# Two-stream feed forward: every low part of the weights on the vector engine, and gate times up written to PSUM

## Chip, cores and metric

One Trainium2 chip, one of its NeuronCores. The metric is the device time of one execution, in microseconds (us), as the median of some runs. The engines are called as the profile calls them: PE (TensorE, matmuls; PEld its weight loads), DVE (VectorE), ACT (ScalarE), POOL (GpSimd) and SP (SyncE, whose queue issues the DMAs).

## The reference, cut to what matters

Two small networks run one after the other on a latent sequence and a context sequence ("streams") of 256 tokens and 1024 features each. Between norms, a convolution module, three attentions and a state space mixer, each has four feed forward layers. In float32:

```
def _swiglu(h, wg, wu, wd):
    return (jax.nn.silu(h @ wg) * (h @ wu)) @ wd          # 1024 -> 2816 -> 1024

def _ffn_half(s, mod, g, wg, wu, wd):
    shift, scale, gate = mod
    h = _modulate(_rmsnorm(s, g), shift, scale)
    return s + 0.5 * gate * _swiglu(h, wg, wu, wd)
...
    ml = (jax.nn.silu(c) @ mod_w[i] + mod_b[i]).reshape(B, 1, N_MOD, D)   # the modulation vectors
```

The state space mixer of the second network needs input, output and transition matrices that depend on weights alone.

## The kernel before

**Split numbers.** A float32 product is made of three matmul passes over rounded operands. Every operand is split into a high part (a rounded copy, made by ACT) and a low part (the number minus its high part, a subtraction). So each weight tile `raw` that arrives by DMA becomes `wh` (ACT, L180) and `wl` (L185), and each activation tile has two parts too: `hh`/`hl` for the input of a layer, `Hh`/`Hl` for the product of gate and up.

**Weight stream.** `pump` runs ahead of PE: it issues the DMA of a chunk of two pieces (L161, on SP's queue), the conversion `wh`, and, when the next piece is converted or the piece is needed, `wl` of the piece before. Five pieces have room. A piece is converted as soon as PE is done with the one five before it. Which engine makes `wl` is decided by the piece's number: every second one by POOL, the others by DVE:

```
            eng = nc.gpsimd if self.n_cv % self.cvm == 1 or self.cv_behind else nc.vector
            self.low()
            self.low_p = lambda eng=eng, l2=l2, r=r, h2=h2: eng.tensor_sub(l2, r, h2.bitcast(F32))
```

**Feed forward** (`ffn`). The 22 tiles of 128 hidden features stand in three groups (6, 8 and 8). In each group PE first makes the gate and up tiles (`gu`, two PSUM tiles for each hidden tile: 48 matmuls over 512 columns, both streams at once), then eight `pd` tiles of the down projection, which read all `Hh` and `Hl` of the group. Between them stands `glu`:

```
                    nc.scalar.activation(out=sg[:, :n], in_=pg[:, :n], func=AF.Silu)
                    pr = sg
                    nc.vector.tensor_mul(pr[:, :n], sg[:, :n], pu[:, :n])
                    hi = Hh[f0 + i][:, c0:c0 + n]
                    nc.scalar.activation(out=hi, in_=pr[:, :n], func=AF.Copy)
                    nc.vector.tensor_sub(Hl[f0 + i][:, c0:c0 + n], pr[:, :n], hi.bitcast(F32))
```

The lines are L774 (`Silu`, ACT), L776 (product, DVE), L778 (`Hh`, ACT) and L779 (`Hl`, DVE). Five PSUM tiles `m` are shared by `gu` and `pd`.

**The eight feed forwards** are called f100, f102, f110 and f112 (first network) and f200, f202, f210 and f212 (second). f112 and f212 have one stream and 256 columns; the other six have two streams.

**Work beside it.** While PE runs a feed forward, DVE makes the modulation vectors of later layers: `jk` (L535), a custom product with a sum over a piece `mw` of the modulation weights. In f100, f102 and f110 the first steps of the state space mixer (`s5_pre`, "the side work") run as well: POOL multiplies small matrices `w` (L2014 to L2024, L2040 to L2050), PE transposes or multiplies them (`pvt`, `kp`), ACT copies them, SP writes them to memory (`dV`), and a later step reuses the buffer. The steps of both are handed out by the matmul time that the program counts, not by what an engine has done. Each engine works through its queue in order. Tile, the framework, orders the instructions of each engine by a simulated run of its own and puts in the waits.

Of the kernel before, what the change touches and what calls it, by code (L numbers as in the profile page):

```python
# [13 lines left out]
D = 1024  # L14
# [13 lines left out]
def pipe(n, stages, lag=1):  # L28
    """stage i of item k goes out lag * i items later, so that no engine stands behind the one before it"""
    for t in range(n + lag * (len(stages) - 1)):  # L30
        for i, f in enumerate(stages):
            if 0 <= t - lag * i < n:
                f(t - lag * i)
# [28 lines left out]
class Task:  # L62
    """background work, one step of a generator every `period` ns of PE time; a step yields the least wait after it"""
# [11 lines left out]
class Core:  # L75
# [39 lines left out]
    def behind(self, ins, prev):  # L115
        """ins is not to be issued before prev"""
        self.tc.add_manual_dep(ins.ins, prev.ins.name, mybir.DependencyInfo(
            mybir.DependencyClass.NoSync, mybir.DependencyReason.DATA), reason="order")

    def behind_pe(self, ins):  # L120
        """ins is not to be issued before the tensor engine has come to where the program is now"""
        self.tc.add_manual_dep(ins.ins, self.last_mm.ins.name, mybir.DependencyInfo(
            mybir.DependencyClass.NoSync, mybir.DependencyReason.DATA), reason="pace")
# [43 lines left out]
    def pump(self):  # L167
        while self.n_cv < min(len(self.pieces), self.n_rel + NBUF):
# [14 lines left out]
            eng = nc.gpsimd if self.n_cv % self.cvm == 1 or self.cv_behind else nc.vector  # L183
# [28 lines left out]
    def gemm(self, out, w, rhs, ks, start=True, stop=True):  # L212
        """w=(hi,lo) pieces [128,nk,128]; rhs(k)->(hi,lo) APs; ks: list of (piece index, rhs key)"""
# [26 lines left out]
    def rstd(self, ch, acc, ncol, eps, cb, d1=900, d2=1500, inv=None, parts=False, pin=0):  # L240
        """acc [128, 128*ncol]: sums over feature tiles, or, parts, the means over each of them in PSUM; cb(bc) with bc [128, 128*ncol] in PSUM."""
# [57 lines left out]
def cols(v):  # L299
    """[n*128] -> [128, n]"""  # L300
# [3 lines left out]
def tiles(w):  # L304
    """[K, M] -> [MT, 128(k), KT, 128(m)]"""
# [53 lines left out]
def na_bias(rpb):  # L359
    """[16, 15, 31] -> [16, 128, 2, 256]: the bias of query (qt, p) and key, -1e30 outside the column window"""  # L360
# [10 lines left out]
def pairs(w):  # L371
    """[K, M] -> [MT/2, 128, 2*KT*128]"""
# [4 lines left out]
def halves(w):  # L377
    """[K, 2M]: tile m of the first half beside tile m of the second -> [MT, 128, 2*KT*128]"""
# [8 lines left out]
def layout(a):  # L387
# [64 lines left out]
    # state space: partition (group parity, state), columns (direction, group pair)  # L452
# [10 lines left out]
    # rows (half, group mod 4, tile in half, group half, h)  # L463
# [5 lines left out]
class Net(Core):  # L469
# [39 lines left out]
    def mods(self, specs):  # L509
        """specs: (b, l, columns, streams_of, then); the sums of every column, then() after the last; a step per sum"""  # L510
# [36 lines left out]
    def begin(self, room):  # L547
        """the first norm, as a generator: feature tile k of both streams goes into hh / hl at step k, as soon as its
        modulation is there; the scale by the vector engine, the shift by the tensor engine"""
# [106 lines left out]
    def prep_norm(self, b, l, n, s):  # L656
        """G = g * (1 + scale)"""
# [43 lines left out]
    def plan_ffn(self, b, l, i, head=0, tail=0):  # L701
        """head, tail: gate/up tiles at the start and down chunks at the end that pass by once for each stream"""
# [12 lines left out]
    def ffn(self, b, streams, ready, gate, after, nsplit=4, first=1, work=None, side=None, head=0, tail=0, begin=None):  # L715
        """ready[s]: chain that fills hh/hl; gate[s]: [128,8] factors; after(s): called once x[s] is done
        (block 1) or y[s] with its sums of squares is done (block 2)."""
        nc, tc = self.nc, self.tc
        two = len(streams) == 2
        N = 512 if two else T  # L720
        with ExitStack() as es:
# [29 lines left out]
            def products(ws, c0, n, last=True, outer=None, step=None):  # L751
                """the gate and up tiles f0, f0 + 1, ... of columns c0:c0 + n; k goes through all of them in turn"""
# [18 lines left out]
            def glu(ps, f0, c0, n):  # L771
                for i, (pg, pu) in enumerate(ps):
                    sg = fp.tile([128, 512], F32, tag="sg", name="sg", bufs=2)
                    nc.scalar.activation(out=sg[:, :n], in_=pg[:, :n], func=AF.Silu)  # L774
                    pr = sg
# [26 lines left out]
            for g, (f0, nf) in enumerate(FGROUPS):  # L802
# [40 lines left out]
                if lastg:  # L843
                    if task is not None:
                        self.drain(task)
                    if side is not None:
                        self.stop(side)
                        self.cvm = 2
# [18 lines left out]
    def proj(self, streams, rhs, epi, ready, after, nk=KT, tiles=1, n=KT, first=1, last=4, again=0):  # L867
        """n outputs of `tiles` weight pieces each; epi(i, s, [psum...]); the first `first` and last `last`
        outputs run one stream after the other, the others for both at once."""
# [49 lines left out]
    def first_tiles(self, ready, streams, n=5):  # L919
        """the first n output tiles, for one stream after the other; gives (j, PSUM tile) as each is done"""  # L920
# [25 lines left out]
    def conv(self, ready, gate, after, NPE=5, NPOOL=8, L=1, n1_=12, n2_=7):  # L946
# [3 lines left out]
        with self.pool("conv") as cp:  # L950
# [23 lines left out]
            def taps(m, ss, n_pe=NPE, n_pool=NPOOL):  # L974
                """v[m]: the taps spread over the tensor engine, the vector engine, and scalar with GpSimd"""
# [171 lines left out]
    def weave(self, a, ta, b, tb, lead=0.0):  # L1147
        """run two generators in turn, in proportion to their PE times ta and tb, b behind a by the part lead"""
# [20 lines left out]
    def na(self, ready, gate, after, NR=1.1, NL=0.2):  # L1169
        nc, tc = self.nc, self.tc  # L1170
        with self.pool("na") as np_, self.pool("na2", 2) as n2:
# [51 lines left out]
            def produce():  # L1223
                """q and k of two heads and, every other time, v of four; at the end the output projection"""
# [32 lines left out]
                # what needs the lat rows only, then the rest of k and v  # L1257
# [34 lines left out]
                # the first output tiles over the heads that are done  # L1292
# [37 lines left out]
            def scores(h, qt, pt, bt):  # L1330
                """softmax of one head and query tile, in pt[:, qt] (SBUF, [128 q, 512 keys])"""
# [26 lines left out]
            def turn(pt, c):  # L1358
                """transpose keys c, c + 1 (of 128) of pt [128 q, 2, keys] into hi and lo [128 keys, q]"""
# [63 lines left out]
    def sums_on_pe(self, n=T):  # L1423
        """a function that takes the squares of feature tile k, and the PSUM tile of its means for rstd"""
# [7 lines left out]
    def post_norm(self, s, acc, gp, sums="vector"):  # L1432
        """x += gp * y * rstd(y); returns the chain and the sums of squares of the new x"""
# [43 lines left out]
    def attn2(self, ready, finish):  # L1477
        """finish(s, acc): y[s] and its sums of squares are done"""
        nc, tc = self.nc, self.tc
        S2 = (LAT, CTX)  # L1480
        with ExitStack() as es:
# [42 lines left out]
            def pe_rope(ps):  # L1524
                """rope of rows 64:96 of ps, with the swapped halves in 96:128, in place"""
# [10 lines left out]
            def rope64(ps):  # L1536
                """rope of both heads' lat columns, in place; rows (half, head)"""
# [8 lines left out]
            # latent projections, then the window attention's q, k, v  # L1546
# [64 lines left out]
            def unit(H, u, ps, p, w, msk):  # L1611
                """exponentials of scores ps [128, w, keys] into p (SBUF), each of the w rows by itself, and their sums"""
# [38 lines left out]
            def score(H, u):  # L1651
                """u = 0, 1: the lat queries of a tile against every key; 2: the ctx queries against the ctx keys"""
# [29 lines left out]
            def pv(H, c):  # L1682
                """the products with the high parts of chunk c, then those with the low parts of the one before"""
# [789 lines left out]
```

## Time and profile before

| | before |
|---|---|
| median of 3 runs (lowest to highest) | 3812.37 us (3811.04 to 3816.39) |
| span of the profiled execution | 3809.8 us |
| mean granted clock of PE | 0.959 |
| PE busy | 3512.7 us (92%) |
| DVE busy | 2733.4 us (72%) |
| ACT busy | 1428.2 us (37%) |
| POOL busy | 1742.2 us (46%) |
| `wl` on POOL | 340 pieces, 2604 ns each |
| `wl` on DVE | 339 pieces, 1422 ns each |
| `Hl` on DVE | 196 tiles, 1482 ns each |
| gate times up on DVE | 196 tiles, 570 ns each |

Busy time is the union of an engine's instructions, and a share is of the span. PE has the largest share, so its idle time, and the stretches in which it runs at a lower granted clock, are what can still be taken out. The profiled execution has no time of its own beside its span; the span lies 2.6 us below the median of the runs.

### The profile page before, as it was taken

To read this page: it belongs to the slowest core of one execution; us is meant where nothing else is said; L and a number is where in the kernel's file an instruction comes from. 1 tells how busy PE (TensorE), PEld (TensorE's weight loads), DVE (VectorE), ACT (ScalarE), POOL (GpSimd) and SP (SyncE) were. 2 spreads that over 40 slices of the span, in tenths; PEclk is the share of its full clock that TensorE was granted. 3 is DMA by queue.
4 is the path that set the end of the run, shared out by engine and by line. 5 is a ranking of instruction groups with operands and counts; after the bars stand their busy time and mean duration, and the time that the engine had idled before them with its cause. 6 is when DMAs were issued, how large, how long until landed. Compare 5 with 4: busy or idle time off the path is not lost. (4 is left out here: it accounts for less than half of the span.)

```text
span 3809.8 us, 55159 instructions
## 1 busy us (share of the span) xinstructions
PE 3512.7 (92%) x21110; PEld 3061.6 (80%) x21110; DVE 2733.4 (72%) x4128; ACT 1428.2 (37%) x2500; POOL 1742.2 (46%) x1255
## 2 busy tenths in 40 slices
PE   8889977899998988998999999888999999998798
PEld 7667755888887776898898888778888888886798
DVE  8889699676659786777998676696666633367665
ACT  4222354533233222455444223465322432233443
POOL 6777556367656676412443223334222422234343
PEclk9999988899999999999999999999999999998899
DMA  6555410255445854423665553102455332238353
GB/s 231 175 193 189 147 55 34 95 170 167 159 142 186 290 198 162 145 95 118 237 238 189 187 177 123 62 28 91 170 183 193 144 111 89 99 122 276 108 183 131
DMA packets 158127, 580.42 MB, mean 152 GB/s; under 512 B 25252, under 2 KB 56740, under 8 KB 118184
## 3 DMA queue, kind: packets, MB, share of 16 engines
q1 hardware_dynamic: 157864, 576.91, 43.6%
q8 instruction: 166, 2.72, 0.3%
q14 instruction: 97, 0.79, 0.1%
HBM read 547.55 MB, written 29.29 MB: 151 GB/s over the span
## 5 line engine op out<-in xcount | busy, mean ns | idle before, releaser
L185 POOL TENSOR_TENSOR wl<-raw,wh 128x1024 fp32r<-128x1024 f32 (+1 forms) x340 | 884.7, 2604 | 1443.7 <-ACT wh L180 1360.9
L180 ACT ACTIVATE wh<-raw 128x1024 fp32r<-128x1024 f32 (+1 forms) x679 | 700.4, 1037 | 1222.5 <-PE gu L106 531.3
L106 PE MATMUL gu<-hl,wh 128*128 128x512 f32 (+1 forms) x3136 | 1085.5, 347 | 9.3 <-DVE hl L693 7.5
L106 PE MATMUL gu<-hh,wl 128*128 128x512 f32 (+1 forms) x3136 | 1084.6, 347 | 8.6 <-DVE wl L185 5.2
L106 PE MATMUL gu<-hh,wh 128*128 128x512 f32 (+1 forms) x3136 | 1080.5, 348 | 7.1 <-ACT hh L690 6.8
L535 DVE CUSTOM_DVE_ANT_0 jk<-mw,cb,vec 128x1024 bf16<-128x1024 f32 x480 | 760.4, 1584 | 38.7 <-DMA mw<-in_mw_dram 24.8
L106 PEld LDWEIGHTS gu<-hl,wh 128*128 128x128 f32 x3136 | 600.7, 192 | 83.9 <-DVE hl L693 9.9
L106 PEld LDWEIGHTS gu<-hh,wl 128*128 128x128 f32 x3136 | 600.4, 192 | 81.8 <-DVE wl L185 6.0
L185 DVE TENSOR_TENSOR wl<-raw,wh 128x1024 fp32r<-128x1024 f32 (+1 forms) x339 | 482.1, 1422 | 252.3 <-ACT wh L180 235.9
L106 PEld LDWEIGHTS gu<-hh,wh 128*128 128x128 f32 x3136 | 598.2, 193 | 80.3 <-ACT hh L690 8.4
L106 PE MATMUL pd<-Hh,wh 128*128 128x256 f32 (+1 forms) x1696 | 567.6, 337 | 24.9 <-ACT Hh L778 23.1
L106 PE MATMUL pd<-Hl,wh 128*128 128x256 f32 (+1 forms) x1696 | 569.3, 336 | 8.4 <-DVE Hl L779 8.4
L106 PE MATMUL pd<-Hh,wl 128*128 128x256 f32 (+1 forms) x1696 | 568.6, 336 | 2.3 <-POOL wl L185 1.9
L106 PEld LDWEIGHTS pd<-Hh,wh 128*128 128x128 f32 x1696 | 326.4, 193 | 59.7 <-ACT Hh L778 26.7
L106 PEld LDWEIGHTS pd<-Hl,wh 128*128 128x128 f32 x1696 | 327.1, 193 | 42.9 <-DVE Hl L779 11.5
L106 PEld LDWEIGHTS pd<-Hh,wl 128*128 128x128 f32 x1696 | 327.6, 193 | 33.7 <-POOL wl L185 2.3
L779 DVE TENSOR_TENSOR Hl<-sg,Hh 128x512 fp32r<-128x512 f32 (+1 forms) x196 | 290.4, 1482 | 45.2 <-ACT Hh L778 45.2
L776 DVE TENSOR_TENSOR sg<-sg,gu 128x512 f32<-128x512 f32 (+1 forms) x196 | 111.6, 570 | 281.2 <-PE gu L106 264.1
L106 PE MATMUL pj<-hh,wh 128*128 128x256 f32 (+1 forms) x736 | 229.6, 328 | 22.1 <-ACT t L967 10.7
L778 ACT ACTIVATE Hh<-sg 128x512 fp32r<-128x512 f32 (+1 forms) x196 | 105.3, 537 | 343.7 <-DVE sg L776 343.3
L106 PE MATMUL pj<-hh,wl 128*128 128x256 f32 (+1 forms) x736 | 230.2, 317 | 0.8 <-DVE wl L185 0.8
L106 PE MATMUL pj<-hl,wh 128*128 128x256 f32 (+1 forms) x736 | 230.0, 317 | 0.6 <-DVE hl L693 0.6
(407 smaller groups left out, 4738.7 us busy)
## 6 DMA issues: line engine op xcount, KB each, us to landing
raw<-in_gu_dram SPq DMA_DIRECT2D x186, 1024.0 KB, 4.8
mw<-in_mw_dram SPq DMA_DIRECT2D x280, 512.0 KB, 4.1
raw<-in_dn2b_dram SPq DMA_DIRECT2D x38, 1024.0 KB, 4.8
raw<-in_dn1b_dram SPq DMA_DIRECT2D x32, 1024.0 KB, 5.5
raw<-in_dn1a_dram SPq DMA_DIRECT2D x16, 768.0 KB, 4.9
raw<-in_pw_dram SPq DMA_DIRECT2D x12, 1024.0 KB, 4.7
raw<-in_dn2a_dram SPq DMA_DIRECT2D x16, 768.0 KB, 4.2
dV<-w SPq DMA_DIRECT2D x32, 256.0 KB, 4.3
```

The costliest lines, as they stand in the source:

```text
L106: ins = self.last_mm = self.nc.tensor.matmul(out=out, lhsT=lhsT, rhs=rhs, start=start, stop=stop, **kw)
L180: ins = nc.scalar.activation(out=h2, in_=r, func=AF.Copy)
L185: self.low_p = lambda eng=eng, l2=l2, r=r, h2=h2: eng.tensor_sub(l2, r, h2.bitcast(F32))
L535: self.behind_pe(nc.vector.tensor_tensor_reduce(out=jk, in0=tl[i], in1=self.cb[s], scale=1.0, scalar=self.V(f"mod_b{b}{l}")[:, j:j + 1], o ...
L776: nc.vector.tensor_mul(pr[:, :n], sg[:, :n], pu[:, :n])
L778: nc.scalar.activation(out=hi, in_=pr[:, :n], func=AF.Copy)
L779: nc.vector.tensor_sub(Hl[f0 + i][:, c0:c0 + n], pr[:, :n], hi.bitcast(F32))
```

## The change

Two edits. In a feed forward of two streams `cvm` is 0, so that every `wl` made while it runs is DVE's; at the end of the last group, ahead of its last pieces, `cvm` is 2 again, and pieces alternate as before. And the product of gate and up is written over `pu`, in PSUM, from where `Hh` and `Hl` are made; this holds for one stream too. Comments and docstrings went as well, which moves some lines by one (L776 is L777 in the changed kernel, L779 is L780).

```diff
-            eng = nc.gpsimd if self.n_cv % self.cvm == 1 or self.cv_behind else nc.vector
+            eng = nc.gpsimd if (self.cvm and self.n_cv % self.cvm == 1) or self.cv_behind else nc.vector
...
     def ffn(self, b, streams, ready, gate, after, nsplit=4, first=1, work=None, side=None, head=0, tail=0, begin=None):
         nc, tc = self.nc, self.tc
         two = len(streams) == 2
         N = 512 if two else T
+        self.cvm = 0 if two else 2
...
-                    pr = sg
+                    pr = pu
                     nc.vector.tensor_mul(pr[:, :n], sg[:, :n], pu[:, :n])
...
                     if side is not None:
                         self.stop(side)
-                        self.cvm = 2
+                    self.cvm = 2
```

The first place is POOL's queue in f110, where the side work makes the matrices `w_11007` and `w_11008` for the products `kp`. Before:

```order
L2024 TENSOR_TENSOR w_10818<-w_10818,w_10819 128x512
L185 TENSOR_TENSOR wl<-raw,wh 128x1024 x2
L2042 TENSOR_TENSOR w_11009<-pw_10677,bc 128x576
L2046 TENSOR_TENSOR w_11008<-pw_10677,bc 128x576
L185 TENSOR_TENSOR wl<-raw,wh 128x1024
L2040 TENSOR_TENSOR w_11007<-pw_10676,bc 128x576
L2044 TENSOR_TENSOR w_11007<-w_11007,w_11009 128x576
```

And in the changed kernel:

```order
L2025 TENSOR_TENSOR w_10818<-w_10818,w_10819 128x512
L2043 TENSOR_TENSOR w_11009<-pw_10677,bc 128x576
L2047 TENSOR_TENSOR w_11008<-pw_10677,bc 128x576
L2041 TENSOR_TENSOR w_11007<-pw_10676,bc 128x576
L2045 TENSOR_TENSOR w_11007<-w_11007,w_11009 128x576
```

The three low parts that stood between the steps are gone; the steps themselves stand in the same order.

The second place is DVE's queue in the second group of f100, from one product of gate and up to the low part of its tile and on to the next product. Before:

```order
L776 TENSOR_TENSOR sg<-sg,gu 128x512
L185 TENSOR_TENSOR wl<-raw,wh 128x1024
L535 ISA jk,mod_211<-mw,cb_245,vec 128x1024
L535 ISA mod_211 128x1
L779 TENSOR_TENSOR Hl_703<-sg,Hh_695 128x512
L535 ISA jk,mod_212<-mw,cb_275,vec 128x1024
L535 ISA mod_212 128x1
L535 ISA jk,mod_211<-mw,cb_245,vec 128x1024
```

In the changed kernel:

```order
L777 TENSOR_TENSOR gu<-sg,gu 128x512
L535 ISA jk,mod_212<-mw,cb_275,vec 128x1024
L535 ISA mod_212 128x1
L185 TENSOR_TENSOR wl<-raw,wh 128x1024
L780 TENSOR_TENSOR Hl_703<-gu,Hh_695 128x512
L535 ISA jk,mod_211<-mw,cb_245,vec 128x1024
L535 ISA mod_211 128x1
...
L185 TENSOR_TENSOR wl<-raw,wh 128x1024
L535 ISA jk,mod_212<-mw,cb_275,vec 128x1024
L535 ISA mod_212 128x1
```

Each hidden tile now has two low parts of weights in DVE's queue in place of one; one `jk` and one `wl` stand between the product and `Hl`, as before.

The third place is DVE's queue near the end of the first group of f100, around `cx`, which overwrites a tile that POOL's powers (`cth`, L1879) read. Before:

```order
L776 TENSOR_TENSOR sg<-sg,gu 128x512
L185 TENSOR_TENSOR wl<-raw,wh 128x768
L535 ISA jk,mod_212<-mw,cb_275,vec 128x1024
L535 ISA mod_212 128x1
L779 TENSOR_TENSOR Hl_707<-sg,Hh_699 128x512
L1925 TENSOR_TENSOR cx<-cli 128x64
```

In the changed kernel:

```order
L780 TENSOR_TENSOR Hl_706<-gu,Hh_698 128x512
L535 ISA jk,mod_211<-mw,cb_245,vec 128x1024
L535 ISA mod_211 128x1
L185 TENSOR_TENSOR wl<-raw,wh 128x768
L535 ISA jk,mod_212<-mw,cb_275,vec 128x1024
L535 ISA mod_212 128x1
L1926 TENSOR_TENSOR cx<-cli 128x64
```

`cx` stands one hidden tile earlier: behind the low part of the group's fourth tile, where it stood behind that of its fifth.

## Rows read from the trace of the kernel before

**Rows 1.** Windows: stretches of f100, f102 (twice), f110, f112, f212.

```profile
core 0: us, PE busy (x) PEld busy (x) DVE busy (x) ACT busy (x) POOL busy (x), PEclk, DMA share, GB/s
110.00:474.70 364.70, 322.42 (x1507) 262.59 (x1505) 297.93 (x450) 92.92 (x138) 251.50 (x199) 0.94 0.52 175
743.20:1126.20 383.00, 377.78 (x2028) 322.12 (x2027) 249.99 (x374) 124.60 (x189) 246.28 (x230) 1.00 0.49 161
819.40:1126.20 306.80, 303.81 (x1499) 253.61 (x1498) 188.42 (x286) 89.50 (x127) 193.80 (x179) 1.00 0.49 161
1126.20:1561.80 435.60, 391.35 (x2034) 328.49 (x2033) 347.14 (x474) 124.26 (x190) 295.47 (x257) 0.95 0.57 199
1779.90:1995.00 215.10, 201.84 (x1592) 198.94 (x1592) 195.24 (x244) 94.12 (x144) 91.92 (x35) 0.95 0.61 220
3605.60:3797.30 191.70, 191.69 (x1584) 191.48 (x1584) 114.70 (x111) 86.64 (x130) 73.44 (x31) 0.99 0.44 154
```

**Rows 2.** PE's waits in f100 from 110 us: us in total, times, longest.

```profile
PE pd L106 <- ACT Hh L778: 14.2, 3, 7.6
PE kp L106 <- POOL w L2044: 8.2, 3, 4.6
PE kp L106 <- POOL w L2050: 5.6, 2, 4.0
PE pd L106 <- DVE Hl L779: 5.0, 3, 2.6
PE pvt L106 <- POOL w L2024: 4.0, 2, 2.3
```

**Rows 3.** PE's waits in f110.

```profile
PE kp L106 <- POOL w L2050: 12.6, 3, 6.7
PE kp L106 <- POOL w L2044: 10.1, 2, 7.7
PE pvt L106 <- POOL w L2018: 9.4, 2, 7.4
```

**Rows 4.** DVE by line in f110: count, busy us, mean ns, idle before.

```profile
L535 DVE CUSTOM_DVE_ANT_0 jk<-mw,cb,vec 128x1024 bf16<-128x1024 f32 x112 | 180.2, 1609 | 32.0 <-DMA mw<-in_mw_dram 22.2 <-ACT cb L506 7.8 <-DVE mod L535 0.5
L185 DVE TENSOR_TENSOR wl<-raw,wh 128x1024 fp32r<-128x1024 f32 x32 | 50.1, 1566 | 0.6 <-ACT wh L180 0.5
L779 DVE TENSOR_TENSOR Hl<-sg,Hh 128x512 fp32r<-128x512 f32 x18 | 28.5, 1582 | 4.5 <-ACT Hh L778 4.5
L776 DVE TENSOR_TENSOR sg<-sg,gu 128x512 f32<-128x512 f32 x18 | 12.3, 681 | 14.6 <-PE gu L106 14.6
```

**Rows 5.** The same view of f200.

```profile
L535 DVE CUSTOM_DVE_ANT_0 jk<-mw,cb,vec 128x1024 bf16<-128x1024 f32 x96 | 140.6, 1465 | 1.4
```

**Rows 6.** POOL by line in f110.

```profile
L185 POOL TENSOR_TENSOR wl<-raw,wh 128x1024 fp32r<-128x1024 f32 (+1 forms) x37 | 104.4, 2825 | 59.1 <-ACT wh L180 58.9
```

**Rows 7.** POOL by line in f200, whose three small groups are left out.

```profile
L185 POOL TENSOR_TENSOR wl<-raw,wh 128x1024 fp32r<-128x1024 f32 (+1 forms) x39 | 104.4, 2679 | 247.8 <-ACT wh L180 239.3 <-DVE Hl L779 3.3 <-DVE wl L185 3.0
```

**Rows 8.** All instructions on tile `jk`: ns min/median/max, first and last start.

```profile
L535 DVE CUSTOM_DVE_ANT_0 jk<-mw,cb,vec x480: 1267/1283/3495, 66.6 to 2949.3; 128x1024 bf16<-128x1024 f32 x160
```

**Rows 9.** Timeline of DVE in f110, while POOL is idle: start, us.

```profile
1324.76 1.22 DVE L185 TENSOR_TENSOR wl<-raw,wh 128x1024 fp32r<-128x1024 f32 x1
```

**Rows 10.** Timeline of POOL in f110; idle time before and its releaser in brackets.

```profile
1331.65 1.17 POOL L2042 TENSOR_TENSOR w<-pw,bc 128x576 f32<-128x576 f32 x1 [12.88 <-DMA dV<-w]
...
1333.89 3.32 POOL L185 TENSOR_TENSOR wl<-raw,wh 128x1024 fp32r<-128x1024 f32 x1
1337.18 2.14 POOL L2040 TENSOR_TENSOR w<-pw,bc 128x576 f32<-128x576 f32 x1
```

**Rows 11.** Timeline of DVE in f100.

```profile
113.92 0.25 DVE L1925 TENSOR_TENSOR cx<-cli 128x64 f32<-128x64 f32 x1 [10.53 <-POOL cth L1879]
```

**Rows 12.** Timeline of POOL in f100.

```profile
90.20 6.17 POOL L185 TENSOR_TENSOR wl<-raw,wh 128x1024 fp32r<-128x1024 f32 x2
...
99.05 14.85 POOL L1879 TENSOR_TENSOR cth<-cx,cr 128x8 f32<-128x8 f32 x8
```

**Rows 13.** DVE by line in f112.

```profile
L779 DVE TENSOR_TENSOR Hl<-sg,Hh 128x256 fp32r<-128x256 f32 x22 | 29.0, 1318 | 0.0
```

## The prediction, made before the result was known

> **What bounds the kernel now.** I first took the busy shares: PE leads with 92%, so the time is PE's work, its waits and its clock. Then I looked at each feed forward by itself, since the edits act there alone. Stretches of PE time are read in the windows view [rows 1]. f102 holds the matmuls of f110 and runs them in 383.0 us at full clock; f110 needs 435.6 us at a mean granted clock of 0.95. f100 from 110 us on (behind its first group's gate and up tiles) takes 364.7 us at 0.94, and the same part of f102 takes 306.8. So 52.6 us in f110 and 57.9 us in f100 are not PE's work. One stream: f112 takes 215.1 us and f212, with the same matmuls, 191.7; 23.4 us more. f102 itself has PE busy for 377.8 of its 383.0 us: next to nothing to win there, and I take f200, f202 and f210, with less work beside them, to be no worse.
>
> Next, PE's own waits in these stretches. In f100 the five largest are 37.0 us: 17.8 for POOL's side work (`kp`, `pvt`) and 19.2 for `Hh` and `Hl`, which the down projection wants as soon as a group ends [rows 2]. In f110 the side work alone makes 32.1 us, up to 7.7 us at a time [rows 3]. The rest of each excess goes with the clock: 6% of 364.7 and 5% of 435.6 us are 22 us each, and full clock in f102 with the same work says that it is the waiting that costs it.
>
> Why is the side work late? The timeline of POOL shows a chain of small products, with 3.32 us of a weight's low part in the middle, which stood in line for nothing that the chain needs, and a product of 2.14 us beside one of 1.17 us of the same shape [rows 10]. POOL spends 104.4 us of f110 on 37 such low parts, and sits blocked for 58.9 us more in front of them, waiting for `wh`, with side work queued behind [rows 6].
>
> And DVE is slowed. `jk` takes 1283 ns in the median of the kernel and 1609 in f110 [rows 8, 4]; a low part takes 1.22 us while POOL is idle and 1566 ns on average [rows 9, 4]; `Hl`, of 512 columns from two SBUF operands, takes 1582 ns, where the product of the same size with one operand in PSUM takes 681 [rows 4].
>
> **Edit 1: all low parts by DVE.** POOL loses 37 pieces in f110, 104.4 us of its 295.5. DVE gets them. Bounds for one: 1.22 us (alone) and 1.57 (as now). How much of today's slowing is due to POOL's low parts, how much to its side work? f200 tells: there POOL does low parts for the same 104.4 us and hardly anything else [rows 7], and 96 `jk` take 1465 ns [rows 5], 17.5 us above 1283 each; in f110 112 of them are 36.5 us above. So about 48% of the slowing goes with the low parts. The other low parts are taken to gain alike: 48% of 0.34 us, hence 1.40 us each. DVE in f110: +37 × 1.40 = 51.8; −17.5 for `jk`; −32 × 0.165 = −5.3 for the low parts that it had.
>
> **Edit 2: the product in PSUM.** The product costs the same: it read PSUM already, and I take writing it there as equal, since no row shows it (bounds: 681 ns, and twice that, 12 us of DVE in f110 with nothing to hide it but DVE's idle time). `Hh` from PSUM is one ACT operand in place of another and ACT is 29% busy in f110, so it is costed at nothing. `Hl` then has one operand in SBUF, the form of the product: 18 × (1582 − 681) = −16.2 us on DVE. The PSUM tile is held longer, until `Hl` is done, some 3 us; five tiles stand in turn, two for each hidden tile, and a hidden tile is 48 matmuls, some 11 us (f102's 306.8 us hold 16 of them and 528 matmuls of the down projection, 0.237 us each), so PE comes back to it much later: nothing. If DVE lay more than that behind, the same time would be waited by PE.
>
> The sum for DVE in f110 is +51.8 − 17.5 − 5.3 − 16.2 = +12.8 us, 347 to 360. I take the same for f100: 298 to 311. DVE is not relieved, it only breaks even; what is gained is POOL's queue.
>
> Beside the row stands a rule of the Trainium skill, "SBUF — State Buffer", section "Who interferes with whom": a DVE instruction with two SBUF inputs and a POOL instruction that reads SBUF hold a shared port one at a time, each for its whole length. By that the side work would block as much per microsecond as the low parts do, and only 104.4/295.5 = 35% of the slowing would go, not 48%: DVE at about +19 us in f110, and some 6 us less gain over both stages. The rows of f200 against f110 decide for 48%, since they compare both kinds of POOL work on this chip.
>
> **From there to PE.**
> - POOL's lateness. In the chain of rows 10 the low part (3.3 us) and the slowed product (1.0) are 4.3 of a 7.7 us wait, but the 12.88 us before it were a wait for the DMA of `dV`, which SP issues behind loads that wait for DVE and POOL. I let two thirds go: 11.9 us of 17.8 in f100, 21.4 of 32.1 in f110.
> - `Hh` and `Hl` late. At the end of f100's first group DVE stood 10.53 us at `cx` [rows 11] for POOL's powers (14.85 us), which had 6.17 us of low parts in front of them [rows 12]; that stall shrinks, though `cx` now stands one tile earlier. But two low parts per tile stand in DVE's queue now. I let a third of 19.2 go: 6.4.
> - Clock: half of 22 us each, 11.
> - New waits in f110, where DVE is fullest in the opening norm: −6, a choice: five low parts at 1.2 us that come in front of the norm.
>
> f100: 11.9 + 6.4 + 11 = 29. Here DVE sets a floor. The busiest that DVE is kept in a stage is 195.2 of 215.1 us, 91%, in f112; 311/0.91 is 342, so I count 23 of the 29. f110: 21.4 + 11 − 6 = 26 (floor 360/0.91 = 396, not reached). f112: DVE bounds it, and `Hl` of 256 columns falls from 1318 ns [rows 13] to at most 681: 22 × 0.64 = 14 us of DVE; I count 9. f102: 2. The sum is 60 us: 3809.8 − 60 = 3749.8 for the span, and 2.6 us more for the median of the runs, 3752. I give 3750.
>
> **Rivals.**
> - The DMAs set the side work's pace. If the waits for `dV` stay, a third of POOL's lateness goes (6 and 11 us) and a quarter of the clock loss (5.5 each): f100 18, f110 11, f112 9, f102 1, together 39: 3773. For it: 12.88 us of idle POOL in front of a 7.7 us wait. Against it: SP stands in line behind the same slow DVE work.
> - All of it goes. Excess 57.9 + 52.6, and 16 of f112: 126, which is 3686. For it: f102 runs the same steps with next to no waits. Against it: f102 has 250 us of DVE work, f110 347.
> - No relief: DVE's slowing belongs to POOL being busy, whatever with, and writing PSUM is slower too. Then f110 has +57.9 − 16.2 = 41.7 more on DVE, 389 us; at 91% that is 427, and f100 366: 8 won, 1 lost, f112 9 won, and 6 to 10 lost to new waits: about 3802, no change. The granularity of the rows speaks against it.
> - Slower: low parts late. All of them now stand in one queue behind `jk` and behind products that wait for PE; a late one stops PE in the middle of a tile, and DVE can't be kept busier than now (80% in f110, 82% in f100). Then f110 needs 360/0.80 = 450 and f100 311/0.817 = 381, 31 us more, less 9 in f112: 3834. It decides from the point where DVE can't pass 83% in f110 (360/435.6) and 85% in f100. Against it: five pieces lie ready, and f112 reaches 91%.
>
> **Numbers.** Forecast (3725 to 3768) 0.45; DMAs set the pace (3768 to 3790) 0.26; all goes (below 3720) 0.14; no change 0.07; slower 0.08. A measurement of this kernel tells about 0.2% from no change, 7.6 us. Faster than that: 0.85; within: 0.07; slower: 0.08. The range that leaves two in ten out is 3697 to 3800: it cuts the far half of "all goes", and what is slower.
>
> **What would show it.** Right: on POOL no low part in the six two-stream feed forwards; `Hl` of 512 columns near 0.68 us in all of them; `jk` in f110 near 1.45 us and low parts on DVE near 1.4; PE's waits for POOL in f110 near 11 us, and f110 near 410 us, f100 from 110 us near 342, f112 near 206. DVE busy about as long as before in f100 and f110. Wrong: waits of PE for `wl` from DVE of more than some 10 us, or waits for `Hh` that grow, would mean that DVE is the bound; waits for `kp` that stay with POOL idle in front of them would mean the DMAs; a product of much over 0.68 us would mean that PSUM costs. f200, f202 and f210 should not move by more than 2 us each.

## The result, and the profile after

The changed kernel takes 3753.86 us (median of 4 runs, 3753.46 to 3762.31) against 3812.98 us for the kernel before (here also 4 runs): a ratio of 0.985, with a 95% interval of 0.984 to 0.986, so 59 us faster. The forecast was 3750. The profiled execution has a span of 3752.0 us against 3809.8. It is 57.8 us shorter; the prediction's sum was 60.

From the page of the changed kernel: the busy time of each engine, and the groups that the change touches.

```profile
span 3752.0 us, 54881 instructions
...
PE 3495.2 (93%) x21110; PEld 3055.5 (81%) x21110; DVE 2652.6 (71%) x4326; ACT 1424.2 (38%) x2500; POOL 1218.5 (32%) x1057
...
L185 DVE TENSOR_TENSOR wl<-raw,wh 128x1024 fp32r<-128x1024 f32 (+1 forms) x537 | 694.1, 1295 | 401.2 <-ACT wh L180 389.8
L185 POOL TENSOR_TENSOR wl<-raw,wh 128x1024 fp32r<-128x1024 f32 (+1 forms) x142 | 360.1, 2537 | 1259.4 <-ACT wh L180 1214.7
L535 DVE CUSTOM_DVE_ANT_0 jk<-mw,cb,vec 128x1024 bf16<-128x1024 f32 x480 | 705.8, 1470 | 29.7 <-DMA mw<-in_mw_dram 19.0
```

The first surprise stands in the DVE column. DVE got 198 more low parts and yet is busy for less time than before (2733 us on the page before). The two edits pull this number two ways: with edit 2 alone (e2 below) DVE is busy for 2600 us, and edit 1 on top of it adds 52.5.

The windows of f100 from 110 us on, f102, f110, f112 and f200, to be held against [rows 1]:

```profile
core 0: us, PE busy (x) PEld busy (x) DVE busy (x) ACT busy (x) POOL busy (x), PEclk, DMA share, GB/s
109.90:446.20 336.30, 310.11 (x1505) 256.45 (x1504) 278.40 (x460) 92.02 (x136) 167.35 (x162) 0.97 0.55 187
716.00:1095.40 379.40, 377.11 (x2028) 322.06 (x2028) 250.34 (x408) 124.85 (x190) 158.13 (x196) 1.00 0.49 163
1095.40:1507.80 412.40, 386.18 (x2035) 326.71 (x2034) 333.72 (x508) 123.69 (x191) 205.98 (x223) 0.97 0.62 210
1725.80:1938.60 212.80, 201.50 (x1593) 198.88 (x1594) 192.44 (x244) 93.55 (x144) 93.61 (x35) 0.95 0.62 223
1938.60:2312.30 373.70, 370.17 (x1993) 322.71 (x1991) 270.14 (x412) 120.50 (x179) 25.14 (x20) 0.99 0.49 170
```

f100 won 28.4 us, f110 23.2, f102 3.6, and f112 only 2.3; f200 lost 2.8, f202 won 2.3, f210 (from the end of f202 on) 4.0. That is 61.0 us; the stretches between them lost the 3.2 that are too many. The mean granted clock rose from 0.94 to 0.97 in f100 and from 0.95 to 0.97 in f110.

DVE by line in f110 (against [rows 4]): mean ns behind the busy time.

```profile
L535 DVE CUSTOM_DVE_ANT_0 jk<-mw,cb,vec 128x1024 bf16<-128x1024 f32 x112 | 164.4, 1468 | 24.7 <-DMA mw<-in_mw_dram 16.7 <-ACT cb L506 6.7
L185 DVE TENSOR_TENSOR wl<-raw,wh 128x1024 fp32r<-128x1024 f32 x62 | 84.5, 1368 | 7.2 <-ACT wh L180 6.7
...
L777 DVE TENSOR_TENSOR gu<-sg,gu 128x512 f32<-128x512 f32 x18 | 12.4, 689 | 7.1 <-PE gu L106 7.1
L780 DVE TENSOR_TENSOR Hl<-gu,Hh 128x512 fp32r<-128x512 f32 x18 | 12.3, 683 | 2.1 <-ACT Hh L779 2.1
```

The two largest groups that read two SBUF operands became shorter: `jk` from 1609 to 1468 ns, a low part from 1566 to 1368. Not all did: `hl` of the layer's input (L693) went from 811 to 841 ns. `Hl`, which now has one operand in PSUM, takes 683 ns. The product that writes PSUM takes 689 ns, against 681 into SBUF.

PE's waits in f100 from 110 us on, and in f110 (us in total, times, longest), against [rows 2, 3]:

```profile
PE pd L106 <- ACT Hh L779: 18.5, 2, 14.8
PE kp L106 <- POOL w L2051: 5.3, 3, 2.3
```

```profile
PE kp L106 <- POOL w L2045: 9.7, 3, 5.1
PE kp L106 <- POOL w L2051: 8.7, 2, 4.8
PE pvt L106 <- POOL w L2019: 4.5, 1, 4.5
```

In f110 the waits for POOL's side work went from 32.1 to 22.9 us, not to 11. In f100 `Hh` still costs 18.5 us, 14.8 of it at one place. The timelines of POOL, ACT and DVE there (start, duration; idle time before it and its releaser in brackets) read as one chain:

```profile
249.53 0.40 POOL L1947 TENSOR_TENSOR pt<-bc,cfr 128x128 f32<-128x128 f32 x1 [29.10 <-DMA bc<-in_s5bc_dram]
```

```profile
250.85 0.31 ACT L2003 ACTIVATE bbz<-bb 64x128 f32<-64x128 f32 x1 [9.23 <-POOL bb L1949]
...
260.01 0.60 ACT L779 ACTIVATE Hh<-gu 128x512 fp32r<-128x512 f32 x1 [4.13 <-DVE gu L777]
```

```profile
252.60 1.23 DVE L185 TENSOR_TENSOR wl<-raw,wh 128x1024 fp32r<-128x1024 f32 x1 [7.20 <-ACT wh L180]
...
259.30 0.68 DVE L777 TENSOR_TENSOR gu<-sg,gu 128x512 f32<-128x512 f32 x1
```

POOL stands idle for 29 us until the load of `bc` lands. ACT is blocked at `bbz` for POOL's result, so `wh` behind it is late; DVE waits for `wh`, the product stands behind that in DVE's queue, and `Hh` behind the product. In the whole run POOL waits 135.8 us for `bc` and 177.5 us for `dV` at L2043, where it waited 61.2 and 87.1 before: it reaches the landings sooner and waits there.

### The profile page after: what moved, and what is told of

It reads as the page before. It is cut to its first block, busy times and chain, and to the rows that moved or that the text cites. A ratio compares the mean times of both kernels' runs of the same rounds, so it can differ in the third digit from the quotient of the medians.

```text
span 3752.0 us, 54881 instructions
## 1 busy us (share of the span) xinstructions
PE 3495.2 (93%) x21110; PEld 3055.5 (81%) x21110; DVE 2652.6 (71%) x4326; ACT 1424.2 (38%) x2500; POOL 1218.5 (32%) x1057
## 5 line engine op out<-in xcount | busy, mean ns | idle before, releaser
L185 DVE TENSOR_TENSOR wl<-raw,wh 128x1024 fp32r<-128x1024 f32 (+1 forms) x537 | 694.1, 1295 | 401.2 <-ACT wh L180 389.8
L185 POOL TENSOR_TENSOR wl<-raw,wh 128x1024 fp32r<-128x1024 f32 (+1 forms) x142 | 360.1, 2537 | 1259.4 <-ACT wh L180 1214.7
L535 DVE CUSTOM_DVE_ANT_0 jk<-mw,cb,vec 128x1024 bf16<-128x1024 f32 x480 | 705.8, 1470 | 29.7 <-DMA mw<-in_mw_dram 19.0
L777 DVE TENSOR_TENSOR gu<-sg,gu 128x512 f32<-128x512 f32 (+1 forms) x196 | 113.2, 578 | 205.5 <-PE gu L106 196.0
L779 ACT ACTIVATE Hh<-gu 128x512 fp32r<-128x512 f32 (+1 forms) x196 | 98.7, 503 | 287.6 <-DVE gu L777 287.6
L106 PEld LDWEIGHTS pj<-hh,wh 128*128 128x128 f32 x736 | 145.5, 206 | 28.9 <-ACT hh L690 8.2
```

Source lines behind the costliest of these rows:

```text
L106: ins = self.last_mm = self.nc.tensor.matmul(out=out, lhsT=lhsT, rhs=rhs, start=start, stop=stop, **kw)
L535: self.behind_pe(nc.vector.tensor_tensor_reduce(out=jk, in0=tl[i], in1=self.cb[s], scale=1.0, scalar=self.V(f"mod_b{b}{l}")[:, j:j + 1], o ...
```

## Experiments

Medians are of 4 runs each; a ratio is always against the kernel before, run on the same chip. On the chips used that kernel took 3813 to 3815 us, and runs of one kernel lie some 3 to 10 us apart, so that a difference of 2 us between two rows says nothing. The first theory was the prediction's: POOL's queue, freed of low parts, lets the side work come earlier, and contention between POOL and DVE is the smaller part.

| run | us | ratio (95%) |
|---|---|---|
| the change | 3753.9 | 0.9849 (0.9836 to 0.9862) |
| e1, edit 1 alone | 3766.3 | 0.9871 (0.9856 to 0.9886) |
| e2, edit 2 alone | 3788.9 | 0.9932 (0.9917 to 0.9947) |
| e3, edit 2, and edit 1 in block 2 | 3786.8 | 0.9925 (0.9910 to 0.9940) |
| e4, the change, one stream too | 3744.1 | 0.9812 (0.9796 to 0.9829) |
| e5, the change, `bc` early | 3740.8 | 0.9805 (0.9791 to 0.9820) |
| e6, the change, POOL does memsets | 3755.6 | 0.9846 (0.9831 to 0.9861) |
| e7, the change, POOL reads SBUF | 3842.1 | 1.0073 (1.0057 to 1.0090) |
| e8, e4 and e5 together | 3730.3 | 0.9777 (0.9762 to 0.9792) |
| e10, the change, POOL waits and does memsets | 3761.5 | 0.9864 (0.9848 to 0.9881) |
| e11, e8, `dV` stored by ACT, one pause less | 3738.7 | 0.9804 (0.9789 to 0.9819) |
| e12, e8, no low part on POOL in the mixers | 3699.4 | 0.9700 (0.9686 to 0.9715) |
| e13, e8, `dV` stored by ACT | 3724.7 | 0.9764 (0.9748 to 0.9780) |

### The two edits apart: e1 and e2

e1 keeps edit 1 and leaves the product in SBUF; e2 keeps edit 2 and gives POOL its half of the low parts back.

```
-                    pr = pu          # e1
+                    pr = sg
```

```
-        self.cvm = 0 if two else 2   # e2
+        self.cvm = 2
```

> Edit 1 alone: all low parts of the two-stream feed forwards on DVE, the product stays in SBUF. Theory (POOL's queue and the contention with POOL make the gain): most of the 59 us is here, 3767 us (3755 to 3780); Hl of 512 columns falls by itself from 1582 ns towards 1.3 us because POOL's low parts are gone; jk in f110 near 1.5 us, f110 near 418, f100 from 110 us on near 342; f112 as before, 215. Rival (the cheaper Hl makes the gain): DVE gets 52 us more in f110 and nothing back, so 3800 us or more.

> Edit 2 alone: the product in PSUM, POOL keeps every second low part. Theory (contention moves to the operations that still read two SBUF operands while POOL works): Hl of 512 columns is near 0.68 us, but jk in f110 rises above its 1609 ns, to 1.7 or more, POOL's waits in f110 stay near 32 us, and the time is 3800 us (3790 to 3808). Rival (the cheaper Hl makes the gain): 16 us less DVE work in each of f110 and f100 and no new waits give 3775 us or less.

Edit 1 alone wins 48 us, edit 2 alone 26, both 59: the two overlap by 15. e1 came as expected in its time and its stretches, and `Hl` fell further than expected, below 1.3 us. e2 won more than my theory gave it and less than the rival's figure. DVE by line in f110 shows both why e2 wins and why the gains overlap, first in e1, then in e2:

```profile
L780 DVE TENSOR_TENSOR Hl<-sg,Hh 128x512 fp32r<-128x512 f32 x18 | 17.9, 992 | 2.2 <-ACT Hh L779 2.2
```

```profile
L535 DVE CUSTOM_DVE_ANT_0 jk<-mw,cb,vec 128x1024 bf16<-128x1024 f32 x112 | 190.2, 1698 | 32.3 <-DMA mw<-in_mw_dram 22.1 <-ACT cb L506 8.7
...
L780 DVE TENSOR_TENSOR Hl<-gu,Hh 128x512 fp32r<-128x512 f32 x18 | 12.3, 682 | 5.6 <-ACT Hh L779 5.6
```

With `Hl` still reading two SBUF operands, taking POOL's low parts away alone brings it from 1582 to 992 ns: two thirds of what edit 2 saves on it was contention, which edit 1 saves too. With edit 2 alone `Hl` is short, but `jk` rises from 1609 to 1698 ns: 112 × 89 ns = 10 of the 16 us saved on `Hl` come back on `jk`. PE's waits for POOL in f110 stay at 31.8 us (12.2, 10.0 and 9.6).

What edit 1 adds to edit 2, 35 us, can't be read from DVE's busy time. The windows row of f110 in e2:

```profile
1114.70:1543.50 428.80, 386.69 (x2035) 326.86 (x2034) 335.24 (x474) 123.33 (x191) 298.94 (x257) 0.96 0.58 202
```

DVE is busy for 335.2 us there and for 333.7 in the changed kernel, with 34 low parts more: what the other operations gain pays for these and no more. Yet f110 is 16.4 us shorter in the changed kernel. That time stands in PE's waits, 42.1 us in all in e2 and 26.1 in the changed kernel: 8.9 less for POOL's side work and 6.3 less for low parts. Whether the side work gains by the queue or by the reads is asked with e6, e7 and e10.

### Where edit 1 acts: e3 and e4

e3 leaves edit 1 in block 2 alone; e4 extends it to the one-stream feed forwards.

```
-        self.cvm = 0 if two else 2
+        self.cvm = 0 if two and b == 2 else 2   # e3
+        self.cvm = 0                            # e4
```

> Edit 2 everywhere, edit 1 in the two-stream feed forwards of block 2 alone (f200, f202, f210); in block 1 POOL keeps every second low part. Theory: the low parts matter where side work stands in POOL's queue, which is block 1, so this is within 6 us of edit 2 alone, about 3797; f200 and f202 stay within 3 us of what they take with edit 2 alone. Rival: the 4.7 us that f210 won is edit 1's and the other two win as much: 10 us or more faster than edit 2 alone.

> The changed kernel, with all low parts on DVE in the one-stream feed forwards f112 and f212 too. Theory (contention is what lengthens jk in f112): 34 low parts of some 1.25 us come to DVE there, 42 us, and 48 jk fall from 1916 ns to near 1.3 us, 30 us, the low parts and sums of squares that it had give 14 more: DVE's busy time stays within 5 us of 192 and f112 within 4 us of 213, the time 3750 to 3758. Rival (DVE's queue is full in f112): DVE rises above 200 us and f112 to 222 or more, 3763 us.

e3 is 2 us from e2: edit 1 wins nothing that shows in block 2. In f200 of the kernel before, PE was busy for 367.9 of 370.9 us, so that the relief of `jk` there (1465 to 1280 ns in the changed kernel) had nothing to win:

```profile
1995.30:2366.20 370.90, 367.94 (x1992) 320.07 (x1991) 261.31 (x380) 120.47 (x179) 112.07 (x52) 1.00 0.49 172
```

e4 wins 10 us more than the change, all of it and more in f112, which falls from 212.8 to 193.0 us. That is far beyond both expectations; the opening of f100 and f200 behind it, 4 us longer each in this execution, took part of it back. The windows row of f112 in e4 and DVE's two largest groups there:

```profile
1733.40:1926.40 193.00, 192.89 (x1593) 192.69 (x1594) 171.75 (x269) 93.79 (x143) 0.70 (x1) 0.99 0.67 235
```

```profile
L185 DVE TENSOR_TENSOR wl<-raw,wh 128x1024 fp32r<-128x1024 f32 x58 | 70.5, 1220 | 8.6 <-ACT wh L180 8.6
L535 DVE CUSTOM_DVE_ANT_0 jk<-mw,cb,vec 128x1024 bf16<-128x1024 f32 x48 | 61.4, 1278 | 0.1
```

The same two groups and POOL's in f112 of the changed kernel:

```profile
L535 DVE CUSTOM_DVE_ANT_0 jk<-mw,cb,vec 128x1024 bf16<-128x1024 f32 x48 | 92.0, 1916 | 0.3
L185 DVE TENSOR_TENSOR wl<-raw,wh 128x1024 fp32r<-128x1024 f32 x29 | 42.9, 1480 | 1.9 <-ACT wh L180 1.8
```

```profile
L185 POOL TENSOR_TENSOR wl<-raw,wh 128x1024 fp32r<-128x1024 f32 x30 | 85.3, 2845 | 105.2 <-ACT wh L180 86.3 <-DVE x L792 8.4 <-PE gu L106 7.1
```

And `jk` in f112 of the kernel before:

```profile
L535 DVE CUSTOM_DVE_ANT_0 jk<-mw,cb,vec 128x1024 bf16<-128x1024 f32 x48 | 77.2, 1608 | 0.3
```

This explains the change's small gain there. Edit 2 took `Hl` of 256 columns from 1318 ns [rows 13] to 415 ns, 22 × 0.90 = 20 us; but POOL's reads were still there, met `jk` in place of `Hl`, and `jk` went from 1608 to 1916 ns, 15 us. In e4 DVE makes 33 more low parts and is busy for 171.75 us, 20.7 less. Worked out: the groups other than low parts take 192.44 − 48.0 = 144.4 us in the changed kernel and 171.75 − 78.1 = 93.7 in e4 (48.0 and 78.1 are the low parts with their pieces of 768 columns, 5.1 and 7.6 us), and DVE's own low parts gain another 9. So 34 low parts on POOL cost DVE some 60 us, 1.75 each. On DVE one takes 1.22. In f112 POOL's help is dearer to DVE than doing the work. In f110 the two are about even, as e2 shows, and over the whole run DVE is busy for 52.5 us more in the change than in e2.

### Queue or reads: e6, e7 and e10

All three give POOL work back in the place of each low part that edit 1 took (e6 and e7 not in f100's first group). It is extra work whose results are used nowhere: in e6 memsets, in e7 subtractions of two SBUF operands, in e10 a wait for `wh`, by a copy of one column of it, and then memsets.

```
+            if self.cvm == 0 and self.n_cv % 2 == 1 and not self.region:
+                for _ in range(4):                               # e6
+                    self.behind(nc.gpsimd.memset(self.idle_t, 0.0), ins)
+                for _ in range(2):                               # e7
+                    self.behind(nc.gpsimd.tensor_sub(self.idle_t, self.idle_t, self.idle_t), ins)
...
+                    nc.gpsimd.tensor_copy(self.idle_t[:, :1], h2[:, :1].bitcast(F32))   # e10
+                    for _ in range(5):
+                        nc.gpsimd.memset(self.idle_t, 0.0)
```

> The changed kernel, and POOL gets work back that reads nothing: for every second piece of the two-stream feed forwards (but those of the first group of f100) four memsets of a scratch tile of 128x512, about the length of one low part of POOL, if a memset takes 0.6 us; it is extra work. Edit 1 on top of edit 2 was worth 35 us. Theory A (POOL's queue: the side work stood behind the low parts): the time goes up by 20 us or more, to 3775 to 3790, with jk of f110 near 1.47 us still. Theory B (the two engines slow each other where both read SBUF): within 6 us of 3754, jk of f110 near 1.47 us, POOL's low parts had cost by their reads.

> The changed kernel, and POOL gets work back that reads two SBUF operands: for every second piece of the two-stream feed forwards (but those of the first group of f100) two subtractions of a scratch tile of 128x512, together the size of one low part; it is extra work, waits for nothing, and its results are used nowhere. Both theories expect a loss, 3780 to 3795 us, with jk of f110 near 1.7 us. Theory A (queue) expects it to lose no more than the memsets do, per microsecond of POOL; theory B (shared reads) 20 us more than the memsets.

> The changed kernel, and POOL stands in line again as it did before, without the reads: for every second piece of the two-stream feed forwards POOL first reads one column of that piece's wh, for which it must wait as its low part did, and then does five memsets of 128x512 (527 ns each in the run with four, so 2.6 us, the length of a low part); it is extra work. Theory A' (what hurt was that the side work stood behind a POOL that waited for wh): 20 us or more lost, 3775 or more, with POOL waiting for ACT's wh in front of these reads for some 50 us in f110. Theory B (the reads slow both engines, the queue hardly matters): within 8 us of 3754.

e6 lost 1.7 us, within its interval, e10 7.6 and e7 88. The windows row of f110 and POOL's added group there, in e6:

```profile
1094.70:1506.80 412.10, 384.80 (x2035) 325.79 (x2034) 333.83 (x508) 123.75 (x191) 265.54 (x359) 0.97 0.62 210
```

```profile
L191 POOL MEMSET idle<- 128x512 f32 x136 | 71.5, 526 | 4.8
```

in e7:

```profile
1126.40:1569.80 443.40, 393.58 (x2035) 329.74 (x2034) 365.40 (x508) 123.55 (x191) 313.32 (x291) 0.95 0.59 195
```

```profile
L191 POOL TENSOR_TENSOR idle<-idle 128x512 f32<-128x512 f32 x68 | 112.8, 1658 | 2.2
```

and in e10, whose memsets and copies together are as long as e7's subtractions (115.4 us and 112.8):

```profile
1106.60:1518.20 411.60, 386.78 (x2034) 327.09 (x2034) 337.36 (x508) 123.58 (x191) 308.46 (x427) 0.97 0.63 210
```

```profile
L193 POOL MEMSET idle<- 128x512 f32 x170 | 89.4, 526 | 7.4
L191 POOL COPY idle<-wh 128x1 f32<-128x1 f32 x34 | 26.0, 765 | 39.8 <-ACT wh L182 39.3
```

The three POOL columns are 265.5, 313.3 and 308.5 us, against 206.0 in the changed kernel. With memsets DVE stays at 333.8 us and f110 at 412; with reads DVE goes to 365.4 and f110 to 443. In e10 POOL is as busy as in e7 and waits 39.3 us for `wh` as well, with all side work behind it, and f110 is 411.6 us. So the runs decide for theory B: POOL's reads beside DVE's cost much, and its queue costs little. The queue's price is the 7.6 us of e10, which lie in f100 (345.5 us against 336.3); it is no strict bound, since POOL waited 58.9 us for `wh` in f110 before [rows 6] and waits 39.3 in e10. Two numbers of e7 were off. I expected 3780 to 3795 us, and it took 3842: the 88 us are not the price of the low parts as they were (edit 1 on top of edit 2 is worth 35), and in e7 DVE makes all low parts as well. And I expected `jk` at 1.7 us and it is 1536 ns, since low parts (1541 ns) and the sums of squares share the loss.

How do the reads reach PE? In f110 in part through the side work, whose lateness I had put down to the queue. PE's waits for it are 38.2 us in e7 and 21.0 in e10; the three longest of each, first e7:

```profile
PE kp L109 <- POOL w L2053: 17.0, 3, 9.4
PE kp L109 <- POOL w L2059: 13.1, 4, 6.3
PE pvt L109 <- POOL w L2027: 6.5, 1, 6.5
```

and e10:

```profile
PE kp L108 <- POOL w L2060: 8.6, 2, 4.7
PE pvt L108 <- POOL w L2028: 6.4, 1, 6.4
PE kp L108 <- POOL w L2054: 5.7, 3, 4.1
```

The steps themselves are not what grew: the 72 products `w` of f110 take 120.9 us before, 122.2 in the changed kernel, 123.0 in e7 and 120.3 in e10. By which way the reads delay the side work stays open.

The Trainium skill says the same of the cause ("SBUF — State Buffer", section "Who interferes with whom"): a DVE instruction with two SBUF inputs contends with a POOL instruction that reads SBUF, and not with one that only writes it. The traces agree, with 776 memsets for 1.7 us, within the interval, and 388 subtractions for 88.

### Landings: e5, e8, e11 and e13

e5 gives `bc` a second buffer and issues its next load behind the store of `dK`; e8 is e4 and e5 in one. e11 issues the stores of `dV` on ACT and drops the pause between copy and store; e13 keeps that pause.

```
-            bc = sp.tile([128, 4, 2, 4, 16], F32, tag="bc", name="bc")
+            bc = sp.tile([128, 4, 2, 4, 16], F32, tag="bc", name="bc", bufs=2)
...
             nc.sync.dma_start(out=self.dK[d], in_=kt)
+            if d < 7:
+                bcs[d + 1] = load(d + 1)
```

```
                     a.activation(out=vt, in_=ps, func=AF.Copy)
-                    yield 2500                # e11 alone
-                    nc.sync.dma_start(out=self.dV[d][r][:, i * 512:i * 512 + 512], in_=vt)
+                    nc.scalar.dma_start(out=self.dV[d][r][:, i * 512:i * 512 + 512], in_=vt)
```

> The changed kernel with a second bc buffer: the load for the next of the eight side-work steps goes out right behind the store of dK of this one, so POOL finds it there. Theory (what POOL waits for now are landings in SP's queue, and these delay PE in f100 and f110): POOL's wait for bc falls from 135.8 us to under 40 and the time to 3742 us (3735 to 3748), f110 to 405. Rival (the wait only moves on to the landing of dV behind it): POOL's wait for dV grows by as much as that for bc falls, and the time stays within 4 us of 3754.

> The low parts of the one-stream feed forwards on DVE too, with the early load of bc: where each gain has a place of its own they add, 3744 less what the early load wins by itself, so 3732 us if that is 12, and 3744 if it is nothing.

> The run with both additions (low parts of the one-stream feed forwards on DVE, bc early), and the stores of dV are issued by ACT right behind the copy that writes their source, no longer by SP behind its loads. Theory (the landing of dV, in SP's line, is what POOL waits for now): POOL's 272 us of waits for dV fall under 100, the 13 us wait of PE for kp in f110 goes, f110 is 397 or less and the time 3720 (3712 to 3726). Rival (the store is late for another reason, or this wait hides behind work): within 4 us of 3730.

> As the run with the stores of dV on ACT, but with the pause between copy and store that the side work's pace had, so that only the issuing engine differs from the run with both additions (3730 us). If the landing of dV held PE up, 3722 us or less. If the earlier run lost by the store standing in ACT's queue (ahead of wh and Hh), as it lost 8 us, 3734 to 3742 again. If it lost by the dropped pause, within 4 us of 3730.

e5 won 13 us, as expected: the wait for `bc` is gone from POOL's list, and half of it moved on to `dV`, which the rival had said. PE's first wait in f100 and POOL's waits in e5:

```profile
PE pd L106 <- ACT Hh L779: 8.5, 3, 3.4
```

```profile
POOL w L2044 <- DMA dV<-w: 250.5, 15, 34.2
...
POOL pt L1947 <- issue: 66.8, 7, 15.6
```

L1947 is the line that had waited for `bc`; 66.8 us of idle time are left in front of it, for which the profile names no releaser. The wait of 14.8 us at `Hh` is gone, and f100 falls from 336.3 to 328.8 us, f110 from 412.4 to 405.5. e8 adds the two gains (10 and 13) in full. e11 fell the wrong way: POOL waits less for `dV`, 148.1 us, and the time is 8 us longer, with 14.1 us of waits for `Hh` in f110. e13 shows that the dropped pause did that: with it the time is 3724.7. That is 6 us under e8, which the intervals can't tell from nothing, and it lies between the two figures expected. POOL's waits for `dV` in e13 and in e11:

```profile
POOL w L2044 <- DMA dV<-w: 248.0, 15, 29.4
```

```profile
POOL w L2043 <- DMA dV<-w: 148.1, 13, 31.7
```

So 100 us of the wait for `dV` go with the pause, by which the side work is let go more slowly, and shortening the wait in this way cost time. That e5's gain comes through `bc` is shown; that `dV` holds anything up is not.

### The rest of the low parts: e12

e12 takes e8 and puts the mixers' low parts, all but two, on DVE as well.

```
-        self.cvm, self.cv_behind = 2, None
+        self.cvm, self.cv_behind = 0, None
...
-                    self.cvm = 2
```

> The run with both additions, and no low part on POOL in the mixers and their projections either: 77 pieces more on DVE. Theory B (a low part on POOL costs by its reads wherever DVE is busy): the mixers have DVE less busy and little to win, so 3722 to 3734. Rival (DVE's queue fills up there): slower than 3736.

It takes 3699 us, 31 less than e8 and 54 less than the change, the fastest of all, and better than I expected by 23. `jk` over the whole of e12:

```profile
L535 DVE CUSTOM_DVE_ANT_0 jk<-mw,cb,vec 128x1024 bf16<-128x1024 f32 x480 | 671.1, 1398 | 19.8 <-DMA mw<-in_mw_dram 10.2 <-ACT cb L506 6.7
```

The gain is spread over the two profiled executions, whose spans are 21.5 us apart: the attention between f200 and f202 takes 269.9 us against 277.8 in e8, f210 376.1 against 381.8, the convolution 266.3 against 270.5, f110 402.1 against 405.7. Part of this is e8's own execution: in the changed kernel that attention took 274.4 us and f210 378.1, with as many low parts on POOL there as in e8. Which waits in the mixers carried the gain was not taken apart.

## Why the prediction was right, and where it was not

The time was right to 4 us, the chief mechanism was not; that the sum came out so close is luck, since errors in its terms cancelled.

- **"What is gained is POOL's queue", and "DVE is not relieved, it only breaks even".** This step failed. DVE in f110 went from 347.1 to 333.7 us, not to 360, and e6 and e10 show that the queue is worth little: what is gained is that POOL no longer reads beside DVE (e7). Edit 2 alone has DVE at 335.2 us already, so "breaks even" is right for edit 1 on top of edit 2, and wrong for both together. The terms: low parts cost DVE 84.5 + 8.8 − 50.1 − 4.7 = +38.5 us (I had +46.5, with 37 pieces, where 34 came into the window); `jk` gave −15.8 (I had −17.5) and `Hl` of 512 columns −16.2, as forecast. Left out were the other operations that meet POOL's reads: `Hl` of 256 columns −4.7, sums of squares −3.0, and small products of the side work and the modulation, some −9. These come to −10; the busy time, which counts a time in which two instructions overlap once, fell by 3 more.
- **"48% of the slowing goes with the low parts".** In f110 `jk` lost 141 of its 326 ns above 1283, 43%; a low part lost 198 of 346, 57%. By the rule of the Trainium skill quoted there ("SBUF — State Buffer", section "Who interferes with whom"), as I had applied it, 35% would have gone (by the steps of my own sum that makes +20 us for DVE, not +19); the rows of f200 were the better guide. In f200, with next to no reads by POOL, `jk` is at 1280 ns.
- **POOL's lateness, "I let two thirds go".** In f110 it went from 32.1 to 22.9 us, 29%, where I had 21.4 us of gain; in f100 the three rows of [rows 2] fell from 17.8 to 7.5, 58%. The path was right, the cause was not: what made the side work late were the reads more than the queue (38.2 us of these waits in e7, 21.0 in e10). For what stayed there is the rival "the DMAs set the pace": POOL waits longer at `bc` and `dV`, and e5 shows 13 us of it.
- **`Hh` and `Hl` late, "a third of 19.2".** 18.7 us are left in f100, and those for `Hh` grew from 14.2 to 18.5, which I had named as a sign that DVE is the bound. It was not that: 14.8 of them hang on the load of `bc`, not on low parts; with that load early (e5) 11.3 are left.
- **The clock, "half of 22 us each, 11".** From 0.94 to 0.97 in f100 and from 0.95 to 0.97 in f110: 3% of 336 and of 412 us are left, 10 and 12, so 12 and 10 were won. This held.
- **The floor in f100 at 342, and the −6 in f110.** Neither was there. DVE was busy for 278 us of f100's 336, and PE's waits outside POOL in f110 shrank. f100 won 28.4, close to the 29 before I cut it to 23, though the 6.4 for `Hh` and `Hl` in it came to 0.5; f110 won 23.2, where I had 26.
- **f112, 9 us.** It won 2.3. The step "`Hl` falls, 14 us of DVE" forgot that POOL's reads would still be there and fall on `jk`: I priced the operation and not the pair of engines. e4 shows the 20 us that were to be had.
- **The product in PSUM.** It costs the same, 689 ns against 681, and `Hh` from PSUM cost nothing that shows (598 ns in f110 against 633).
- **f200, f202 and f210 within 2 us each.** They moved by +2.8, −2.3 and −4.0. e2 has f210 at 378.3 us as the change has it, so that gain is edit 2's.

So the sum had too much for POOL's lateness, for f112 and for the stall at `Hh`, and it took off too much for a DVE that would be the bound: 6 us in f100 by the floor and 6 in f110 for new waits.

## What to carry to other kernels

When two engines share work, price the pair: here POOL's reads lengthened what DVE does with two SBUF operands, and moving an operation from one engine to the other can cost the other next to nothing. In f112 a low part on POOL cost DVE 1.75 us and one on DVE 1.22; in f110 the two were about even. It pays where the slowed engines hold up the bound one: in f110 and f112 it did, in block 2, where PE was busy nearly all the time, it won nothing that shows. Taking one victim out of the way (`Hl` through PSUM) moves part of the collision to the next (`jk`) as long as the reads stay, so first take away the reader, and test a queue theory with fill work that occupies the queue and reads nothing.

## What the runs showed of the hardware that was not expected

- A memset of 128x512 on POOL takes 526 ns and slows DVE by nothing that shows: 71.5 us of them in f110 leave DVE at 333.8 us against 333.7.
- `jk` has no slowing of its own: it is at 1278 to 1280 ns in f112 of e4 and in f200 of the change, where POOL reads next to nothing, and at 1916 ns beside POOL's low parts.
- A copy of one column (128x1) on POOL took 765 ns in f110.
